# A hybrid decoder trunk on one core: the opening stage in strict order of its pieces, the squares of x behind it, and the statistics' product one chunk later

## The chip, the cores and the metric

The kernel runs on one core of a Trainium2 chip. The metric is the device time of one execution in microseconds (us). The engines are TensorE (PE in the profile, its weight loads PEld), VectorE (DVE), ScalarE (ACT), GpSimd (POOL) and SyncE (SP), which issues the DMAs here. Each engine works through its own queue in order.

## The reference

One layer, for a sequence of 256 positions and a width of 1024, all float32:

```
h    = rms_norm(x) * g_mix
proj = h @ w_in                      # columns: attention q,k,v; second attention q,k,v; rx, rgate; 3 gates
xr   = causal_dwconv(rx, width 4)    # the recurrent branch starts from the columns rx
...
x    = x + merged @ w_out
x    = x + (gelu(u_gate) * u_val) @ ffn_down     # u = conv3(rms_norm(x) @ ffn_up)
out  = rms_norm(x)
```

What matters here is the beginning: `rms_norm` divides every position by the root of the mean square over the 1024 channels, and the first columns of the product that the kernel takes are those of `rx`. The division by the root can be done after the product, since it is one factor for each position.

## The kernel before, in words

Everything is held transposed: 128 channels on the partitions, 256 positions along the free axis, so x is 8 tiles of 128 x 256, called k = 0 to 7. A float32 product is made of three matmuls on fp32r parts: each operand is split into a high part (a ScalarE copy that rounds) and a low part (a VectorE subtraction), and `mm3` (L109) adds high·high (L110), high·low (L111) and low·high (L112). So each tile of x needs a pair of instructions (`scaled_split`, L162: L164 on ScalarE, L165 on VectorE, called xgh and xgl), and each tile of weights needs one too (whi on ScalarE, wlo on VectorE).

The weights come in 77 chunks of 1 MB in the order ORDER. Chunks 0 and 1 are special: they hold the first half of the rx columns, cut by k, so that the work can begin when the first pieces of x and of the weights are there. SP issues those pieces alternately (L122 to L132): weights for k = 0, x for k = 0, and so on; from k = 2 on a DMA carries two k. Then come the parameters, chunk 2 (L86) and two small vectors. The raw chunks have three buffers; the split halves of chunks (1024 columns) have four.

The opening stage is the loop of L200: for every k, split x's tile k, split the 512 columns of weights of that k (L209, L210; in two parts for k = 0), and make 12 matmuls into two PSUM banks `rxb` (96 in all). Behind the loop stand, in program order: the split of chunk 2 (`split_to(6)`, L96 and L97, halves 4 and 5); the squares of x (`sumsq_bcast`, L186: four ScalarE instructions over two tiles each) and their sum (L188: two additions on GpSimd, then one on VectorE); the product of that sum with a matrix of ones (`sumsq_mm`, L194 and L195), which puts the sum over all channels on every partition; `rstd_of` (L169 to L173: one ScalarE and four VectorE instructions), which makes the factor `rstd1`; the evacuation of the two banks (`rx_evac`, L262), which multiplies by `rstd1`; and chunks 2 and 3 (`T_chunk`, 48 matmuls and one bank each), tied behind the statistics' product on TensorE. The pool of banks `psA` has four: rxb0, rxb1, then one for each chunk, so chunk 4 takes the bank of rxb0 again.

The order of the instructions on each engine is not that of the program. The framework schedules them: of what it thinks ready it takes what comes first in the program. The block `with tc.issue_after(i)` puts every instruction that it holds, and that runs on the engine of `i`, behind `i`. This sets an order on that engine and adds no wait on another one. In the kernel before, the opening loop has no such block, and the squares have none either. A chain of some 25 tiny GpSimd instructions over 8 columns (L290 to L304, tile `sm`) also runs in this stretch.

Of the kernel before, what the change touches and what calls it, by code (L numbers as in the profile page):

```python
# [8 lines left out]
F32 = mybir.dt.float32  # L9
F32R = mybir.dt.float32r  # L10
AF = mybir.ActivationFunctionType
ALU = mybir.AluOpType

P = 128
S = 256
D = 1024
KD = D // P
# [42 lines left out]
def hybrid_trunk(ctx: ExitStack, tc: tile.TileContext, x, wts, par, rgw, lqk, gf, out):  # L60
    nc = tc.nc
    V, A, G, T = nc.vector, nc.scalar, nc.gpsimd, nc.tensor
# [9 lines left out]
    def mm_bank(name):  # L72
        return psA.tile([P, 512], F32, name=name, tag="mm")

    def at_bank(name):
        return psB.tile([P, 512], F32, name=name, tag="at")


    raws, his, los = {}, {}, {}
    state = {"load": 0, "split": 0}  # L80

    def load_to(n):
        while state["load"] < min(n, NCHUNK):
            i = state["load"]
            raws[i] = rawp.tile([P, CH], F32, name=f"raw{i}", tag="raw")
            nc.sync.dma_start(raws[i], wts[i])  # L86
            state["load"] += 1

    def split_to(n):

        while state["split"] < min(n, 2 * NCHUNK):
            i = state["split"]
            raw = raws[i // 2][:, (i % 2) * HC:(i % 2 + 1) * HC]
            his[i] = wsp.tile([P, HC], F32R, name=f"whi{i}", tag="whi")
            los[i] = wsp.tile([P, HC], F32R, name=f"wlo{i}", tag="wlo")
            A.activation(his[i], raw, AF.Copy)  # L96
            V.tensor_tensor(los[i], raw, his[i].bitcast(F32), ALU.subtract)  # L97
            state["split"] += 1

    def half(i, e, name):  # L100
        assert ORDER[i][0] == name, (i, ORDER[i], name)
        load_to(i + RAW_BUFS)
        split_to(2 * i + e + W_BUFS)
        return his.pop(2 * i + e), los.pop(2 * i + e)
# [4 lines left out]
    def mm3(ps, wh, wl, ah, al, start, stop, **kw):  # L109
        T.matmul(ps, lhsT=wh, rhs=ah, start=start, stop=False, **kw)  # L110
        T.matmul(ps, lhsT=wh, rhs=al, start=False, stop=False, **kw)  # L111
        T.matmul(ps, lhsT=wl, rhs=ah, start=False, stop=stop, **kw)  # L112
# [4 lines left out]
    xt = xg_in[:, KD:].rearrange("p (k s) -> p k s", k=KD)  # L117
    gmix = xg_in[:, 0:KD]
# [20 lines left out]
    def pc(name, j, n=1):  # L139
        return par_s[:, PC[name] + j:PC[name] + j + n]  # L140
# [18 lines left out]
    xgh = big.tile([P, KD, S], F32R, name="xgh", tag="s1")  # L159
    xgl = big.tile([P, KD, S], F32R, name="xgl", tag="s2")  # L160

    def scaled_split(hi, lo, src, gain, ks):  # L162
        for k in ks:
            A.activation(hi[:, k, :], src[:, k, :], AF.Copy, scale=gain[:, k:k + 1])  # L164
            V.scalar_tensor_tensor(lo[:, k, :], src[:, k, :], gain[:, k:k + 1], hi[:, k, :].bitcast(F32),  # L165
                                   op0=ALU.mult, op1=ALU.subtract)

    def newton(y, m, t, r, ss_ap, scale):
        A.activation(y, ss_ap, AF.Abs_reciprocal_sqrt, bias=eps_s, scale=scale)  # L169
        V.tensor_scalar(m, ss_ap, -0.5 * scale, -0.5 * EPS, op0=ALU.mult, op1=ALU.add)  # L170
        V.tensor_tensor(t, y, y, ALU.mult)
        V.tensor_tensor(t, m, t, ALU.mult)
        V.scalar_tensor_tensor(r, t, 1.5, y, op0=ALU.add, op1=ALU.mult)  # L173

    def rstd_of(ss_ap, n, scale, name):

        m = work.tile([P, n], F32, name=name + "m", tag="nt_m", bufs=1)
        y = work.tile([P, n], F32, name=name + "y", tag="nt_y", bufs=1)
        t = work.tile([P, n], F32, name=name + "t", tag="nt_t", bufs=1)
        r = work.tile([P, n], F32, name=name + "r", tag="rstd", bufs=1)  # L180
        newton(y, m, t, r, ss_ap, scale)
        return r

    def sumsq_bcast(sq, k, src, name, later=False):

        A.activation(sq[:, k:k + 2, :], src[:, k:k + 2, :], AF.Square)  # L186
        if k:
            (G if k < 6 else V).tensor_tensor(sq[:, 0:2, :], sq[:, 0:2, :], sq[:, k:k + 2, :], ALU.add)  # L188
        if k == 6 and not later:
            return sumsq_mm(sq, name)  # L190

    def sumsq_mm(sq, name):
        ps = at_bank(name + "ss")
        T.matmul(ps[:, :S], lhsT=ones, rhs=sq[:, 0, :], start=True, stop=False)  # L194
        return ps[:, :S], T.matmul(ps[:, :S], lhsT=ones, rhs=sq[:, 1, :], start=False, stop=True)  # L195

    rx_banks = [mm_bank(f"rxb{b}") for b in range(2)]
    for k in range(KD):  # L200
        scaled_split(xgh, xgl, xt, gmix, [k])
        if k % 2 == 0:
            his[k // 2] = wsp.tile([P, HC], F32R, name=f"whi{k // 2}", tag="whi")
            los[k // 2] = wsp.tile([P, HC], F32R, name=f"wlo{k // 2}", tag="wlo")
        wh = his[k // 2][:, (k % 2) * 512:(k % 2 + 1) * 512]
        wl = los[k // 2][:, (k % 2) * 512:(k % 2 + 1) * 512]
        raw = raws[k // 4][:, (k % 4) * 512:(k % 4 + 1) * 512]
        for c in (slice(0, 256), slice(256, 512)) if k == 0 else (slice(0, 512),):
            A.activation(wh[:, c], raw[:, c], AF.Copy)  # L209
            V.tensor_tensor(wl[:, c], raw[:, c], wh[:, c].bitcast(F32), ALU.subtract)  # L210
        for t in range(4):
            mm3(rx_banks[t // 2][:, (t % 2) * S:(t % 2 + 1) * S], wh[:, t * P:(t + 1) * P], wl[:, t * P:(t + 1) * P],
                xgh[:, k, :], xgl[:, k, :], start=(k == 0 and t % 2 == 0), stop=(k == KD - 1 and t % 2 == 1),
                skip_group_check=True)
    state["split"] = 4
    load_to(4)
    split_to(6)
    sq1 = big.tile([P, KD, S], F32, name="sq1", tag="s7")
    for k in range(0, KD, 2):
        ss1 = sumsq_bcast(sq1, k, xt, "n1")  # L220
    ss1, ss1_mm = ss1
    rstd1 = rstd_of(ss1, S, 1.0 / D, "n1")
    gffn = pc("gffn", 0, 8)

    G.iota(dist, pattern=[[-1, S]], base=P, channel_multiplier=1, allow_small_or_imprecise_dtypes=True)
# [3 lines left out]
    def T_chunk(i, name, ah, al, evac, nk=KD, kouter=False):  # L229

        nt = HC // (nk * P)
        ps = None
        if kouter:
            hv = [half(i, e, name) for e in range(2)]
            ps = mm_bank(f"mm{i}")
            for k in range(KD):
                for t in range(2):
                    w = slice(k * P, (k + 1) * P)
                    mm3(ps[:, t * S:(t + 1) * S], hv[t][0][:, w], hv[t][1][:, w], ah[:, k, :], al[:, k, :],
                        start=(k == 0 and t == 0), stop=(k == KD - 1 and t == 1), skip_group_check=True)  # L240
            evac(ps, ORDER[i][1] * 2)
            return
        for e in range(2):
            wh, wl = half(i, e, name)
            wh4 = wh.rearrange("p (t k c) -> p t k c", k=nk, c=P)
            wl4 = wl.rearrange("p (t k c) -> p t k c", k=nk, c=P)
            for t in range(nt):
                o = (e * nt + t) % 2
                if o == 0:
                    ps = mm_bank(f"mm{i}_{e}{t}")  # L250
                for k in range(nk):
                    mm3(ps[:, o * S:(o + 1) * S], wh4[:, t, k, :], wl4[:, t, k, :],
                        ah[:, k, :], al[:, k, :], start=(k == 0), stop=(k == nk - 1))
                if o == 1:
                    evac(ps, ORDER[i][1] * 2 * nt + e * nt + t - 1)

    SP = S + 3
    rx = big.tile([P, KD, SP], F32, name="rx", tag="s5")
    G.memset(rx[:, :, 0:3], 0.0)

    def rx_evac(ps, t):
        V.tensor_tensor(rx[:, t:t + 2, 3:], ps.rearrange("p (t s) -> p t s", t=2),  # L262
                        rstd1[:, None, :].to_broadcast([P, 2, S]), ALU.mult)
# [10 lines left out]
        A.activation(hh[:, s, :], hf[:, s, :], AF.Copy)  # L274
        V.tensor_tensor(hl[:, s, :], hf[:, s, :], hh[:, s, :].bitcast(F32), ALU.subtract)

    rx_evac(rx_banks[0], 0)
    rx_evac(rx_banks[1], 2)
    pos = 2
    for c in range(2):  # L280
        with tc.issue_after(ss1_mm.ins):
            T_chunk(pos, "rx", xgh, xgl, rx_evac)
        pos += 1


    sm = const.tile([P, 12, 8], F32, name="sm")
# [398 lines left out]
    sq1 = big.tile([P, KD, S], F32, name="sq1b", tag="s1")  # L685
# [71 lines left out]
    for name, idx in FFN_ORDER:  # L757
        if name == "up":
            raw = idx < RAW_UP
# [11 lines left out]
        else:  # L771
# [3 lines left out]
            last = NFF // 2 - 1  # L775
# [7 lines left out]
            for h, c, i, e in ([(h, c, i, e) for h in range(2) for c in range(2) for i in (last - 1, last)  # L783
# [4 lines left out]
                ps = dn_banks[h][c]  # L788
# [81 lines left out]
```

## Time and profile before

| | |
|---|---|
| time, median of three runs | 483.67 us (483.54 to 484.66) |
| the profiled execution | 483.25 us, span 481.1 us |
| PE busy | 469.9 us (98%), 3580 matmuls |
| DVE busy | 382.6 us (80%) |
| ACT busy | 305.4 us (63%) |
| POOL busy | 19.7 us (4%) |
| mean granted TensorE clock | 0.997 of full speed |

The span begins and ends inside the execution, so its time is a little longer than the span. Busy time is that of instructions, so an engine that waits for a semaphore is idle. A matmul's end is modelled: matmuls overlap in the records (0.28 us each, starting 0.12 us apart), and the steady rate is read from their starts.

### The profile page before, as it was taken

The page shows a single profiled execution, that of the slowest core. Times are in us where ns is not written, and L with a number is a line of the kernel's source. Part 1 is how long each engine was busy: PE and PEld are TensorE (multiplying, and loading weights), DVE is VectorE, ACT ScalarE, POOL GpSimd, SP SyncE. Part 2 cuts the span into 40 slices and gives each one's busy share as a digit, 9 for nine tenths or more (in the row PEclk, how much of TensorE's full clock was granted, in tenths as well). Part 3 has the DMA queues.
Part 4 walks back from the last instruction along what each step waited for, and adds up shares of the span by engine and source line. Part 5 has one row for each costly group of instructions (what it writes and reads, how often), then busy time and mean ns, then how long its engine had stood idle before and what let it go on. Part 6 is the DMA issues. An engine that isn't in the chain of part 4 may idle for free.

```text
span 481.1 us, 8975 instructions
## 1 busy us (share of the span) xinstructions
PE 469.9 (98%) x3580; PEld 451.1 (94%) x3580; DVE 382.6 (80%) x686; ACT 305.4 (63%) x517; POOL 19.7 (4%) x46
## 2 busy tenths in 40 slices
PE   6999999999999999999999999999999999999994
PEld 5999999989999999999999999999999999999983
DVE  4899979657877599979567787999887788678575
ACT  6756739567778895576454556867565556555562
POOL 2640000000000000000000020000000000000000
PEclk9999999999999999999999999999999999999998
DMA  8954996998452525556654555455655445555302
GB/s 258 360 198 182 274 276 236 250 218 322 168 174 89 175 80 184 187 193 231 253 187 176 219 176 174 177 181 181 229 195 178 175 176 184 180 195 187 131 1 89
DMA packets 20395, 92.61 MB, mean 192 GB/s; under 512 B 1921, under 2 KB 8833, under 8 KB 10625
## 3 DMA queue, kind: packets, MB, share of 16 engines
q1 hardware_dynamic: 20352, 92.03, 56.2%
q8 instruction: 28, 0.46, 0.4%
q14 instruction: 15, 0.11, 0.1%
HBM read 84.69 MB, written 1.05 MB: 178 GB/s over the span
## 4 chain that ended last, share of the span: by engine, by line
PE 95%; ACT 1%; DMA 1%; DVE 1%; issue 0%; SPq 0%; DVEq 0%
PE mm L110 24%; PE mm L111 24%; PE mm L112 24%; PE dn L789 4%; PE dn L790 4%; PE dn L791 4%; DMA raw<-in_wts_dram 1%; PE va L450 1%; PE vc L448 1%; PE va L448 1%; PE va L449 1%; PE vc L450 1%; PE vc L449 1%; PE oa L498 0%; PE rxb L112 0%; PE rgg L110 0%
## 5 line engine op out<-in xcount | busy, mean ns | idle before, releaser
L96 ACT ACTIVATE whi<-raw 128x1024 fp32r<-128x1024 f32 x150 | 158.2, 1058 | 121.6 <-PE mm L111 87.1
L97 DVE TENSOR_TENSOR wlo<-raw,whi 128x1024 fp32r<-128x1024 f32 x150 | 182.6, 1220 | 50.6 <-ACT whi L96 49.1
L110 PE MATMUL mm<-x1h,whi 128*128 128x256 f32 x320 | 90.9, 284 | 0.0
L110 PE MATMUL mm<-hh,whi 128*128 128x256 f32 x320 | 90.9, 284 | 0.0
L112 PE MATMUL mm<-hh,wlo 128*128 128x256 f32 x320 | 90.5, 283 | 0.0
L111 PE MATMUL mm<-hl,whi 128*128 128x256 f32 x320 | 90.5, 283 | 0.0
L111 PE MATMUL mm<-x1l,whi 128*128 128x256 f32 x320 | 90.3, 282 | 0.0
L112 PE MATMUL mm<-x1h,wlo 128*128 128x256 f32 x320 | 89.7, 280 | 0.0
L110 PEld LDWEIGHTS mm<-hh,whi 128*128 128x128 f32 x320 | 61.3, 192 | 0.1
L111 PEld LDWEIGHTS mm<-hl,whi 128*128 128x128 f32 x320 | 61.3, 192 | 0.0
L112 PEld LDWEIGHTS mm<-hh,wlo 128*128 128x128 f32 x320 | 61.3, 192 | 0.0
L112 PEld LDWEIGHTS mm<-x1h,wlo 128*128 128x128 f32 x320 | 61.0, 191 | 0.0
L111 PEld LDWEIGHTS mm<-x1l,whi 128*128 128x128 f32 x320 | 60.7, 190 | 0.2
L110 PEld LDWEIGHTS mm<-x1h,whi 128*128 128x128 f32 x320 | 60.2, 188 | 0.2
L789 PE MATMUL dn<-whi,act 128*128 128x512 f32 x88 | 34.5, 392 | 0.0
L790 PE MATMUL dn<-wlo,act 128*128 128x512 f32 x88 | 34.4, 391 | 0.0
L791 PE MATMUL dn<-whi,act 128*128 128x512 f32 x88 | 34.3, 390 | 0.0
L110 PE MATMUL mm<-xgh,whi 128*128 128x256 f32 x96 | 27.0, 282 | 0.0
L111 PE MATMUL mm<-xgl,whi 128*128 128x256 f32 x96 | 26.9, 280 | 0.0
L112 PE MATMUL mm<-xgh,wlo 128*128 128x256 f32 x96 | 26.9, 280 | 0.0
L707 ACT ACTIVATE cv<-us,par_s 128x256 f32<-128x256 f32 x40 | 21.6, 588 | 0.0
L717 ACT ACTIVATE act<-cv 128x256 fp32r<-128x256 f32 x22 | 9.1, 412 | 17.4 <-DVE cv L713 17.4
(476 smaller groups left out, 1016.5 us busy)
## 6 DMA issues: line engine op xcount, KB each, us to landing
raw<-in_wts_dram SPq DMA_DIRECT2D x75, 1024.0 KB, 4.8
raw<-in_wts_dram SPq DMA_DIRECT2D x3, 512.0 KB, 6.6
KSa<-kha SPq DMA_DIRECT2D x4, 256.0 KB, 5.6
KLa<-qka SPq DMA_DIRECT2D x4, 256.0 KB, 6.3
KSc<-khc SPq DMA_DIRECT2D x4, 256.0 KB, 5.9
KLc<-klc SPq DMA_DIRECT2D x4, 256.0 KB, 8.7
rgw<-in_rgw_dram SPq DMA_DIRECT2D x2, 512.0 KB, 11.3
xt<-in_x_dram SPq DMA_DIRECT2D x1, 1024.0 KB, 7.1
```

The lines of the kernel that those rows point to most:

```text
L96: A.activation(his[i], raw, AF.Copy)
L97: V.tensor_tensor(los[i], raw, his[i].bitcast(F32), ALU.subtract)
L110: T.matmul(ps, lhsT=wh, rhs=ah, start=start, stop=False, **kw)
L111: T.matmul(ps, lhsT=wh, rhs=al, start=False, stop=False, **kw)
L112: T.matmul(ps, lhsT=wl, rhs=ah, start=False, stop=stop, **kw)
L448: T.matmul(banks[s], lhsT=hs, rhs=wh3[:, kk], start=(k == 0), stop=False)
L449: T.matmul(banks[s], lhsT=hs, rhs=wl3[:, kk], start=False, stop=False)
L450: T.matmul(banks[s], lhsT=ls, rhs=wh3[:, kk], start=False, stop=(k == 7))
L707: A.activation(cv[:, e, :], src[:, o:o + S], AF.Identity, bias=pc("fb", ch), scale=pc("fw", 88 + ch))
L789: T.matmul(ps, lhsT=hi, rhs=hv[i][e][0][:, o], start=(i == 0 and e == 0), stop=False)
L790: T.matmul(ps, lhsT=hi, rhs=hv[i][e][1][:, o], start=False, stop=False)
L791: T.matmul(ps, lhsT=lo, rhs=hv[i][e][0][:, o], start=False, stop=(i == last and e == 1))
```

## The change

Three things are altered. In the opening loop a list `last` holds the last ScalarE and the last VectorE instruction of the piece before, and the splits of piece k are issued behind them, so both engines take the pieces strictly in the order of k. The split of chunk 2 is put behind piece 7 and the squares behind the split of chunk 2 in the same way. And the statistics' product, with `rstd_of` and the evacuation of the two banks, moves behind the matmuls of chunk 2, whose own evacuation is kept in a list (`late`) and done after theirs; chunk 3 is tied behind the product.

```diff
@@ split_to @@
-            A.activation(his[i], raw, AF.Copy)
-            V.tensor_tensor(los[i], raw, his[i].bitcast(F32), ALU.subtract)
+            state["a"] = A.activation(his[i], raw, AF.Copy)
+            state["v"] = V.tensor_tensor(los[i], raw, his[i].bitcast(F32), ALU.subtract)
@@ opening stage @@
+    last = []
+
+    def behind():
+        es = ExitStack()
+        for i in last:
+            es.enter_context(tc.issue_after(i))
+        return es
+
     for k in range(KD):
-        scaled_split(xgh, xgl, xt, gmix, [k])
...
-        for c in (slice(0, 256), slice(256, 512)) if k == 0 else (slice(0, 512),):
-            A.activation(wh[:, c], raw[:, c], AF.Copy)
-            V.tensor_tensor(wl[:, c], raw[:, c], wh[:, c].bitcast(F32), ALU.subtract)
+        with behind():
+            scaled_split(xgh, xgl, xt, gmix, [k])
+            for c in (slice(0, 256), slice(256, 512)) if k == 0 else (slice(0, 512),):
+                a_ = A.activation(wh[:, c], raw[:, c], AF.Copy)
+                v_ = V.tensor_tensor(wl[:, c], raw[:, c], wh[:, c].bitcast(F32), ALU.subtract)
+        last[:] = [a_.ins, v_.ins]
...
     load_to(4)
-    split_to(6)
+    with behind():
+        split_to(6)
+    last[:] = [state["a"].ins, state["v"].ins]
     sq1 = big.tile([P, KD, S], F32, name="sq1", tag="s7")
-    for k in range(0, KD, 2):
-        ss1 = sumsq_bcast(sq1, k, xt, "n1")
-    ss1, ss1_mm = ss1
-    rstd1 = rstd_of(ss1, S, 1.0 / D, "n1")
+    with behind():
+        for k in range(0, KD, 2):
+            sumsq_bcast(sq1, k, xt, "n1", later=True)
...
-    rx_evac(rx_banks[0], 0)
-    rx_evac(rx_banks[1], 2)
     pos = 2
-    for c in range(2):
-        with tc.issue_after(ss1_mm.ins):
-            T_chunk(pos, "rx", xgh, xgl, rx_evac)
-        pos += 1
+    late = []
+    T_chunk(pos, "rx", xgh, xgl, lambda ps, t: late.append((ps, t)))
+    ss1, ss1_mm = sumsq_mm(sq1, "n1")
+    rstd1 = rstd_of(ss1, S, 1.0 / D, "n1")
+    for b, t in [(rx_banks[0], 0), (rx_banks[1], 2)] + late:
+        rx_evac(b, t)
+    pos = 3
+    with tc.issue_after(ss1_mm.ins):
+        T_chunk(pos, "rx", xgh, xgl, rx_evac)
+    pos = 4
```

## Rows read from the trace of the kernel before

**Rows 1.** Window 21 to 60: length, busy us (instructions) of each engine, PE clock, DMA share, GB/s.

```profile
21.00:60.00 39.00, 39.00 (x312) 38.09 (x311) 36.68 (x62) 25.78 (x34) 7.75 (x18) 1.00 0.68 233
```

**Rows 2.** All waits of PE in the span: us in total, times, longest.

```profile
PE rxb L110 <- ACT whi L209: 2.1, 3, 1.0
PE warm L147 <- DVE eps_s L149: 1.0, 1, 1.0
PE rxb L112 <- DVE wlo L210: 0.8, 2, 0.7
```

**Rows 3.** Timeline of PE: start, us, engine, line, operation, tiles, [idle before <- releaser].

```profile
11.76 0.39 PE L112 MATMUL rxb<-xgh,wlo 128*128 128x256 f32 x1 [0.67 <-DVE wlo L210]
...
14.36 0.28 PE L111 MATMUL rxb<-xgl,whi 128*128 128x256 f32 x1
14.80 0.39 PE L112 MATMUL rxb<-xgh,wlo 128*128 128x256 f32 x1 [0.16 <-DVE wlo L210]
...
20.36 0.60 PE L194 MATMUL n1ss<-sq,ones 128*128 128x256 f32 x2
...
21.35 0.28 PE L111 MATMUL mm<-xgl,whi 128*128 128x256 f32 x1
...
32.50 0.28 PE L110 MATMUL mm<-xgh,whi 128*128 128x256 f32 x1
```

**Rows 4.** Timeline of ACT in the opening.

```profile
8.66 1.14 ACT L186 ACTIVATE sq<-xg_in 128x512 f32<-128x512 f32 x2
9.70 1.14 ACT L209 ACTIVATE whi<-raw 128x512 fp32r<-128x512 f32 x2
10.74 0.89 ACT L164 ACTIVATE xgh<-xg_in 128x256 fp32r<-128x256 f32 x2
...
12.06 1.14 ACT L209 ACTIVATE whi<-raw 128x512 fp32r<-128x512 f32 x2
...
14.42 1.13 ACT L209 ACTIVATE whi<-raw 128x512 fp32r<-128x512 f32 x2
...
16.71 2.01 ACT L96 ACTIVATE whi<-raw 128x1024 fp32r<-128x1024 f32 x2 [0.82 <-DMA raw<-in_wts_dram]
18.74 1.28 ACT L169 ACT_TABLE_LOAD   x1
21.43 0.47 ACT L169 ACTIVATE n1y<-n1ss,eps_s 128x256 f32<-128x256 f32 x1 [1.40 <-PE n1ss L195]
```

**Rows 5.** Timeline of DVE in the opening, single instructions and pairs.

```profile
10.35 1.36 DVE L210 TENSOR_TENSOR wlo<-raw,whi 128x512 fp32r<-128x512 f32 x1 [1.01 <-ACT whi L209]
...
12.63 1.52 DVE L165 SCALAR_TENSOR_TENSOR xgl<-xg_in,xgh 128x256 fp32r<-128x256 f32 x1
14.07 1.28 DVE L210 TENSOR_TENSOR wlo<-raw,whi 128x512 fp32r<-128x512 f32 x2
15.28 0.87 DVE L165 SCALAR_TENSOR_TENSOR xgl<-xg_in,xgh 128x256 fp32r<-128x256 f32 x2
...
18.01 1.21 DVE L97 TENSOR_TENSOR wlo<-raw,whi 128x1024 fp32r<-128x1024 f32 x1
...
25.70 1.28 DVE L262 TENSOR_TENSOR rx<-rxb,n1r 128x512 f32<-128x512 f32 x2
```

**Rows 6.** Timeline of POOL.

```profile
9.88 1.28 POOL L188 TENSOR_TENSOR sq<-sq 128x512 f32<-128x512 f32 x1 [6.97 <-ACT sq L186]
...
12.30 1.57 POOL L188 TENSOR_TENSOR sq<-sq 128x512 f32<-128x512 f32 x1 [1.08 <-ACT sq L186]
...
18.15 1.13 POOL L292 TENSOR_TENSOR sm<-sm 128x8 f32<-128x8 f32 x1 [1.90 <-DVE lam_s L314]
...
30.05 0.23 POOL L304 TENSOR_SCALAR sm<-sm 128x8 f32<-128x8 f32 x1
```

**Rows 7.** SP's issue of the weights for k = 2 and 3.

```profile
3.53 0.43 SPq L132 DMA_DIRECT2D raw<-in_wts_dram  x1
```

**Rows 8.** DMA issues at 3.5 to 3.9: size, us from issue to landing.

```profile
raw<-in_wts_dram SPq DMA_DIRECT2D x1, 512.0 KB, 5.6
```

## The prediction

> **What bounds the kernel now.** I read the stretches first, then what PE waits for, then the timelines of the opening. From 21 us on PE is busy without a gap at full granted clock, 39.00 of 39 us in the first such stretch [rows 1], and the list of PE's waits over the whole span names nothing but the opening: 2.1 us for high parts of weights, 0.8 us for low parts, 1.0 us before the warm-up [rows 2]. So PE sets the end, and after the opening every later matmul follows the one before. A microsecond that the opening gives PE comes out at the end, as long as no new wait takes it; work taken from ACT, DVE or POOL elsewhere is worth nothing.
>
> In the opening, the reader should look at the two matmuls that begin after a wait for a low part, at 11.76 and 14.80 us [rows 3]. From 14.80 to the statistics' product at 20.36 there are the last 46 of the 96 matmuls: 5.56 us, that is 46 at 0.1185 and 0.11 for the restart. From 11.76 to 14.36 the same rate gives 22 more starts and the next one would have come at 14.48. So 68 matmuls follow 11.76, and 28 (k = 0, 1 and four of k = 2) came before.
>
> Why is the low part of k = 2 late? Two reasons. ACT makes two squares, 8.66 to 9.80, while the weights for k = 2 and 3 (issued at 3.53, landed 5.6 later, at 9.13) lie ready; their high part begins at 9.70 instead [rows 4, 7, 8]. And DVE needs 1.36 us for the low part, 10.35 to 11.71, where a free one takes 0.68 (a pair 1.28, so 0.60 apart) [rows 5]: GpSimd's addition of those squares runs from 9.88 to 11.16 [rows 6]. The second addition, 12.30 to 13.87, does the same to the x part of k = 5 (1.52 us; a free pair takes 0.87) and makes the low weights of k = 4 late, the wait at 14.80.
>
> **The change: the opening.** Four squares (0.52 apart) leave ACT's opening and three additions leave POOL's and DVE's; nothing is added there, and no DMA is moved. ACT begins the high part of k = 2 at 9.15 and ends it at 9.77; DVE makes the low part at 9.79 to 10.47, and PE goes on at 10.52 (it started 0.05 after the low part's end before) instead of 11.76: 1.24 us. For k = 3, ACT needs 0.52 and 0.40 more, so its high part ends at 10.69 and the low one at 11.47; PE wants that at 10.52 + 0.11 + 8 x 0.1185 + 0.24 = 11.82. The pieces k = 4 and 5 follow at 1.00 us each on DVE (0.60 + 0.40) against PE's 1.42, so the margin grows, as long as the weights have landed. They had by 12.06 for k = 4 and by 14.42 for k = 6, where ACT took them straight after other work [rows 4]; from there the low parts would be ready at 13.35 and 15.71, and PE wants them at 13.24 and 16.08. For k = 4 that latest case costs 0.2; I take none, since 12.06 stood behind a square. So the wait at 14.80 goes too: 14.80 - 14.48 + 0.11 = 0.43. PE ends the opening at 10.52 + 0.11 + 68 x 0.1185 = 18.69 instead of 20.36: **1.67 us**. Bounds: nothing, if PE meets another late piece; and 2.1 us, if it had all four late matmul groups of k = 2 in hand and lost neither the wait nor the restart.
>
> **The change: chunk 2 comes too early.** Its weights do not come earlier: ACT stood idle 0.82 us for their landing and began at 16.71 [rows 4]. One high half takes 1.06, its low part on a free DVE 1.21 [rows 5]: 17.79 to 19.00, at PE 19.05. PE, now without the statistics in between, wants the first low part with the third matmul of chunk 2, at 18.69 + 2 x 0.1185 = 18.93. So it stands 0.12 and restarts for 0.11: **0.23 us given back**. That landing is a ceiling: however soon the opening ends, chunk 2 can't pass 19.05 with its third matmul. Only another order of chunk 2's matmuls, high parts first, would lift it; then up to the whole 1.67 stays. The chunk's rate is (32.50 - 21.35)/95 = 0.1174 [rows 3], so its 48 matmuls are through at 19.05 + 0.23 + 45 x 0.1174 = 24.56.
>
> **The change: the statistics.** The product costs the same at its new place: from 20.36 to the second matmul of the next chunk at 21.35 are 0.99 us where 0.12 are due, so 0.87 before and after. What must hold is that the sum of squares is there by 24.56. ACT ends half 5 at 18.72 and then squares: the second ends near 19.8, the fourth near 20.8. GpSimd's first addition finds DVE on the low part of half 5 (18.95 to 20.16); the two additions then take 20.2 to 22.7 at 1.28 each, and DVE's addition ends at 23.4. If DVE puts one split of chunk 3 (1.21) ahead of it, 24.5. Either is just in time: **0**, with bounds of 0 and about 1.1 us (two splits ahead, 25.7).
>
> The Trainium skill, "SBUF — State Buffer", section "Who interferes with whom", says that a VectorE instruction with two SBUF inputs and a GpSimd instruction that reads SBUF exclude each other wholly, whoever comes first. The trace agrees: the low part of k = 2 ends 0.55 us after GpSimd's addition, and the second addition took 1.57 behind a VectorE instruction instead of 1.28 [rows 5, 6]. By that rule GpSimd waits for half 5 as I have it; were they to share, half 5 would be some 0.4 us later, before PE needs it near 22, so the sum stays at 0 either way.
>
> Then the factor: from the product's end, ACT's root began at 21.43, which is 1.07 after 20.36, and the first bank was free at 25.70 + 0.68 = 26.38 [rows 4, 5], 4.95 us later. Now: 24.56 + 1.07 = 25.63 and 30.58. Chunk 4 takes that bank at 24.56 + 0.87 + 48 x 0.1174 = 31.07. It holds by 0.5 us: **0**; bounds 0 and 0.7 (one more split of 1.21 in between). The third evacuation and the later weight splits are covered by PE's chunks of 5.6 us. The table load in front of the root (1.28 us [rows 4]) lies in ACT's time before 25.63.
>
> **Sum.** 1.67 - 0.23 - 0 - 0 = 1.44 us off the profiled execution's 483.25, so 481.81. The median of the runs is 0.42 above it, so 483.67 - 1.44 = 482.23. That is 0.30% under the time before, and 0.3% (1.45 us) is about what a measurement of this kernel can tell from no change. The likeliest case lies on that line.
>
> **Rivals.**
>
> 1. *The statistics' product waits.* GpSimd or DVE take other work ahead of the additions, as the tiny chain that has one of 1.13 us at 18.15 [rows 6]. PE then stands before chunk 3. One or two such pieces: 0.3 to 1.4 us lost, 482.5 to 483.6. For it: the margin is 0.1 to 1.2 us. Against it: the additions come first in the program.
> 2. *Chunk 2 is ordered with its high parts first*, or its landing is a little earlier: 1.67 to 2.0 us gained, 481.7 to 482.0. For it: four matmuls of k = 2 stood ahead of its first low one. Against it: at k = 4, where 46 of 48 follow the wait at 14.80, the low one stands third again.
> 3. *The bank is late.* The root is held up and chunk 4 waits for bank 0. A delay of 1.2 us on ACT or DVE costs 0.7: 482.9. The Trainium skill, "ScalarE: Activation LUTs", section "What ACT_TABLE_LOAD costs", counts about 2.66 us with the drain for a switch of tables; the row shows 1.28 with 0.02 before it, and if the load cost as the page has it, 1.38 more would leave this rival's loss at up to 0.9.
> 4. *Slower: GpSimd runs the whole tiny chain first.* It lasted from 18.15 to 30.28 [rows 6]. With two additions and DVE's behind it, the sum would come near 33.5, the product 9 us late, and the time be 7.5 us above the one before, 491. It decides from a sum later than 24.56 + 1.44 = 26.0. Against it: two squares are ready near 19.8, 1.7 us after that row, and of what is ready the earlier in the program is taken; it comes true only if the scheduler's idea of that moment is far off.
> 5. *No change:* a piece other than the squares holds PE, and the opening ends near 20.3: 483.7.
>
> **How the numbers follow.** The forecast (481.8 to 482.7 alone) 0.50; rival 1, 0.20; rival 2, 0.11; rival 3, 0.06; rival 4 and other losses beyond 0.3%, 0.09; rival 5, 0.04. Faster by over 0.3%: rival 2 and a little over half of the forecast, 0.39. Slower 0.09. Within 0.3%: the rest, 0.52. The range 481.3 to 484.0 holds all but rival 4 and takes in the spread of the runs.
>
> **What the profile would show.** ACT takes xgh, whi of each k in turn with no square before 18.7; whi of k = 2 begins near 9.15; no low split in the opening is over 0.7 us; PE's wait at 14.80 is gone and its last rxb matmul starts near 18.6; a short wait for L97 stands at 19; the product starts near 24.6 without a wait and chunk 4 near 31.1. A wait of the product for DVE's addition speaks for rival 1 or 4, one of chunk 4 for L262 for rival 3, none at 19 for rival 2. The prediction is wrong if GpSimd's additions don't stand right behind the squares, or if a raw landing has moved.

## The result and the profile after

The changed kernel is slower: 487.23 us in the median of 22 runs (484.92 to 488.75), beside 484.39 for the kernel before on the same chips; the ratio is 1.0054, with an interval of 1.004 to 1.0068. The ratios here and below are taken over the fast runs of both kernels, so they differ a little from the quotients of the medians. The prediction was 482.2, with a range of 481.3 to 484.0. Rival 4, which had a chance of 0.09 with its like, is what happened, at a lower price than its 491. The profiled execution took 487.29 us with a span of 485.2 and a mean granted clock of 0.994, against 483.25, 481.1 and 0.997 before.

All waits of PE in the kernel after, as [rows 2] (us in total, times, longest):

```profile
PE n1ss L194 <- DVE sq L188: 3.5, 1, 3.5
PE rxb L110 <- ACT whi L219: 1.2, 2, 0.9
PE warm L147 <- DVE eps_s L149: 1.0, 1, 1.0
```

The opening's own waits have shrunk: the low parts (0.8 us before) are gone from the list and the high parts fell from 2.1 to 1.2. But a new wait of 3.5 us stands at the head, and it is the statistics' product that waits for VectorE's addition. The lines of the split are now L219 and L220 (L209 and L210 before), the tiny chain is L307 to L321 (L290 to L304 before). The timeline of PE, as [rows 3]:

```profile
10.60 0.38 PE L112 MATMUL rxb<-xgh,wlo 128*128 128x256 f32 x1
...
18.86 0.28 PE L112 MATMUL rxb<-xgh,wlo 128*128 128x256 f32 x1
18.98 0.28 PE L110 MATMUL mm<-xgh,whi 128*128 128x256 f32 x1
...
19.25 0.38 PE L112 MATMUL mm<-xgh,wlo 128*128 128x256 f32 x1
...
24.63 0.28 PE L112 MATMUL mm<-xgh,wlo 128*128 128x256 f32 x1
28.43 0.70 PE L194 MATMUL n1ss<-sq,ones 128*128 128x256 f32 x2 [3.52 <-DVE sq L188]
```

Up to 24.63, the last matmul of chunk 2, things go nearly as the prediction had them: PE goes on at 10.60 (10.52 forecast), chunk 2's first low part is in use at 19.25 (19.05), and chunk 2 is through at 24.63 + 0.12 = 24.75 (24.56). Then PE stands still. Who is late is seen on three engines. ACT, as [rows 4], makes the high part of k = 2 at 9.19 with no square in front, and its squares right behind chunk 2's high parts:

```profile
9.19 0.63 ACT L219 ACTIVATE whi<-raw 128x512 fp32r<-128x512 f32 x1 [0.94 <-DMA raw<-in_wts_dram]
...
16.87 2.01 ACT L96 ACTIVATE whi<-raw 128x1024 fp32r<-128x1024 f32 x2 [1.08 <-DMA raw<-in_wts_dram]
18.79 2.18 ACT L186 ACTIVATE sq<-xg_in 128x512 f32<-128x512 f32 x4
...
29.93 0.47 ACT L169 ACTIVATE n1y<-n1ss,eps_s 128x256 f32<-128x256 f32 x1 [2.75 <-PE n1ss L195]
```

The four squares are done at 20.97. POOL, as [rows 6], doesn't take them up:

```profile
16.78 0.20 POOL L309 TENSOR_TENSOR sm<-sm 128x8 f32<-128x8 f32 x1 [0.32 <-DVE sm L308]
...
18.23 1.02 POOL L313 TENSOR_TENSOR sm<-sm 128x8 f32<-128x8 f32 x1
19.34 1.08 POOL L314 TENSOR_SCALAR sm<-sm 128x8 f32<-128x8 f32 x1
20.51 0.20 POOL L313 TENSOR_TENSOR sm<-sm 128x8 f32<-128x8 f32 x1
...
24.73 0.23 POOL L321 TENSOR_SCALAR sm<-sm 128x8 f32<-128x8 f32 x1
25.04 2.61 POOL L188 TENSOR_TENSOR sq<-sq 128x512 f32<-128x512 f32 x2
```

It runs the tiny chain to its end at 24.96 and only then the two additions, though the last of all squares was there 4 us earlier. DVE, as [rows 5], shows the end of the delay:

```profile
9.86 0.69 DVE L220 TENSOR_TENSOR wlo<-raw,whi 128x512 fp32r<-128x512 f32 x1 [1.09 <-ACT whi L219]
...
16.49 0.20 DVE L308 RECIPROCAL sm<-sm 128x8 f32<-128x8 f32 x1
17.96 2.37 DVE L97 TENSOR_TENSOR wlo<-raw,whi 128x1024 fp32r<-128x1024 f32 x2 [1.27 <-ACT whi L96]
27.68 0.69 DVE L188 TENSOR_TENSOR sq<-sq 128x512 f32<-128x512 f32 x1 [7.35 <-POOL sq L188]
```

VectorE's own addition stands in its queue ahead of the splits of chunk 3, so the engine waits 7.35 us for POOL and the whole queue stands with it. And there is a second loss behind the first. Stretches of the span (length, busy time and count of PE, PEld, DVE, ACT and POOL, granted clock, DMA share, GB/s):

```profile
26.00:28.00 2.00, 0.00 (x0) 0.00 (x0) 0.32 (x1) 1.19 (x1) 1.57 (x2) 1.00 0.03 12
28.00:29.00 1.00, 0.57 (x3) 0.52 (x4) 1.00 (x2) 0.00 (x0) 0.00 (x0) 1.00 0.00 0
29.00:32.00 3.00, 3.00 (x14) 2.82 (x13) 3.00 (x4) 0.47 (x1) 0.00 (x0) 0.51 0.09 11
32.00:33.00 1.00, 1.00 (x9) 1.00 (x8) 1.00 (x2) 0.00 (x0) 0.00 (x0) 0.75 0.80 270
33.00:60.00 27.00, 27.00 (x228) 26.91 (x227) 26.36 (x47) 18.05 (x25) 0.00 (x0) 1.00 0.65 213
```

From 29 to 32 us PE is busy all the time, but the granted clock is 0.51, the lower of its two levels (1.2 GHz), and 14 matmuls start where a full clock has room for 26. Before the fall the engine had stood still for 3.52 us. From 33 on the clock is full and PE busy without a gap, as in [rows 1].

**Where the time went.** By the starts of PE's last matmul (473.59 before, 478.04 after) the loss is 4.45 us. Chunk 2 is through at 24.75 instead of 26.87 - 0.87 = 26.00, if the product that lay before it is taken out: 1.25 gained. The product starts at 28.43 instead of 24.75: 3.68 lost. From the product to the last matmul are 449.61 us, where the first experiment below, at full clock, has 447.95: 1.66 lost. Nearly all of it lies in the first chunk: from the product's start to that of the 48th matmul behind it are 8.10 us here and 6.45 there. The remaining 0.36 lies in the later chunks (before has 453.23 - 48 x 0.1174 = 447.59), and the tail behind the last matmul is 0.35 shorter, so the two nearly cancel in the span.

### The profile page after: what moved, and what is told of

It reads as the page before. It is cut to its first block, busy times and chain, and to the rows that moved or that the text cites. A ratio compares the mean times of both kernels' runs of the same rounds, so it can differ in the third digit from the quotient of the medians.

```text
span 485.2 us, 8979 instructions
## 1 busy us (share of the span) xinstructions
PE 472.6 (97%) x3580; PEld 453.5 (93%) x3580; DVE 381.0 (79%) x686; ACT 305.5 (63%) x517; POOL 15.6 (3%) x46
## 4 chain that ended last, share of the span: by engine, by line
PE 93%; POOL 2%; DMA 2%; ACT 1%; SPq 1%; DVE 1%; issue 1%; DVEq 0%; POOLq 0%
PE mm L110 23%; PE mm L111 23%; PE mm L112 23%; PE dn L806 4%; PE dn L807 4%; PE dn L808 4%; DMA raw<-in_wts_dram 2%; PE va L465 1%; PE vc L466 1%; PE vc L467 1%; PE va L466 1%; PE vc L465 1%; PE va L467 1%; POOL sq L188 1%; POOL sm L314 1%
## 5 line engine op out<-in xcount | busy, mean ns | idle before, releaser
L110 PE MATMUL mm<-xgh,whi 128*128 128x256 f32 x96 | 28.0, 291 | 0.0
```

## The experiments

Each ran beside runs of the kernel before on the same chip. Two reasons for the loss were to be told apart: POOL's order, with the chain in front of the additions (theory A), and something in the new place of the product or the strict order itself (rival). The first two experiments keep the strict order and the later product as they are and alter only the order of POOL's work or the engine of the additions.

**The chain behind the additions.** The changed kernel, with the whole block of the tiny chain tied behind GpSimd's last addition.

```diff
+            state["g" if k < 6 else "s"] = (G if k < 6 else V).tensor_tensor(
+                sq[:, 0:2, :], sq[:, 0:2, :], sq[:, k:k + 2, :], ALU.add)
...
+    with tc.issue_after(state["g"].ins):
+        A.activation(sm[:, 0], lam_c, AF.Abs)
...
```

> The changed kernel, with the chain of small GpSimd instructions (tile sm) put behind GpSimd's second addition of squares; nothing else moves. Theory A (the loss is GpSimd's queue: the additions stood behind the whole chain, PE waited 3.52 us for the sum, and the clock then fell): the additions run at about 20 to 22.7 us, the sum is there by 24.5, PE's product starts near 24.75 without a wait, the clock stays full, and the time is 1.0 to 1.4 us under the kernel before (ratio 0.997 to 0.998), some 4 us under the changed kernel. Rival B (the later product itself costs, by the factor and the banks coming late, whoever makes the sum): PE's wait moves to chunk 4 and the kernel stays 1 us or more slower than before.

Measured: 482.03 us (481.03 to 482.80, 12 runs) beside 484.79 (482.96 to 489.87, 33 runs); ratio 0.9925, interval 0.9896 to 0.9953. POOL's timeline of this run, and below it PE's:

```profile
20.25 2.85 POOL L188 TENSOR_TENSOR sq<-sq 128x512 f32<-128x512 f32 x2 [17.29 <-ACT sq L186]
```

```profile
25.00 0.59 PE L195 MATMUL n1ss<-sq,ones 128*128 128x256 f32 x2
```

The additions come 4.8 us earlier, the product runs without a wait, and the granted clock is 1.00 from 24 to 60 us. The loss is gone, and the gain of the opening is seen. The ratio is lower than the 0.997 to 0.998 that was expected, since the runs of before spread far upwards; the two profiled executions, 482.19 and 483.25, lie 1.06 us apart, as expected. Against the changed kernel the gain is plain: the slowest run here, 482.80, is below its fastest, 484.92.

**All additions on VectorE.** The changed kernel again; now the chain keeps its place at the head of POOL, and the additions leave POOL.

```diff
-            (G if k < 6 else V).tensor_tensor(sq[:, 0:2, :], sq[:, 0:2, :], sq[:, k:k + 2, :], ALU.add)
+            (V if name == "n1" else G if k < 6 else V).tensor_tensor(
+                sq[:, 0:2, :], sq[:, 0:2, :], sq[:, k:k + 2, :], ALU.add)
```

> The changed kernel, with all three additions of the first statistics on VectorE; the chain stays where it is on GpSimd. Theory A: VectorE, which stood idle from 20.3 to 27.7 us, adds at 0.68 us each behind the squares, the sum is there near 21.6, no wait at the product, full clock, ratio 0.997 to 0.998 as with the chain moved. If the port between GpSimd and VectorE were the cause and not the order of GpSimd's queue, the chain beside it would still make the additions late, and a wait of 1 us or more stays.

Measured: 481.73 (480.71 to 481.86, 10 runs), ratio 0.9912, interval 0.9878 to 0.9946. This is the fastest version of the study, and its slowest run lies below the fastest of the 33 of before. DVE and PE in this run:

```profile
20.14 2.27 DVE L188 TENSOR_TENSOR sq<-sq 128x512 f32<-128x512 f32 x3
22.38 3.73 DVE L97 TENSOR_TENSOR wlo<-raw,whi 128x1024 fp32r<-128x1024 f32 x3
```

```profile
24.71 0.59 PE L195 MATMUL n1ss<-sq,ones 128*128 128x256 f32 x2
```

The chain was as early as in the changed kernel and did no harm, so it is its place in front of the additions, not the chain, that cost the time. Two edits that have only this in common both win back more than the loss, with the strict order and the later product in place and no wait of chunk 4 in either run: theory A stands, and the rival falls.

**The wait filled with matmuls.** To price the clock by itself: the changed kernel with 14 matmuls of `ones` by `ones` between chunk 2 and the product. They are work added, and their result isn't used.

```diff
...
-    ss1, ss1_mm = sumsq_mm(sq1, "n1")
+    fill = at_bank("fill")
+    with tc.issue_after(state["mm"].ins):
+        for _ in range(14):
+            fl = T.matmul(fill[:, 0:P], lhsT=ones, rhs=ones, start=True, stop=True)
+    with tc.issue_after(fl.ins):
+        ss1, ss1_mm = sumsq_mm(sq1, "n1")
...
```

> The changed kernel, with 14 matmuls of ones by ones (128 columns, result unused) between chunk 2 and the statistics' product, so that PE works through most of its wait of 3.5 us. The sum comes as late as before. Theory A1 (the 3.4 us at half clock after the wait are a price of PE's idleness): the clock stays full and the time falls by about 1.7 us against the changed kernel (half of 3.4). Rival (the slow matmuls behind the wait come from something else, such as the float32 product itself or VectorE's four splits at that time): they stay slow, and the time stays that of the changed kernel.

Measured: 486.58 (485.71 to 490.42, 12 runs), ratio 1.0036, interval 1.0004 to 1.0067. Its stretch from 29 to 32 us, and its waits of PE:

```profile
29.00:32.00 3.00, 3.00 (x27) 3.00 (x26) 3.00 (x4) 0.57 (x2) 0.00 (x0) 1.00 0.17 44
```

```profile
PE a0s L484 <- issue: 1.2, 1, 1.2
...
PE n1ss L194 <- DVE sq L188: 0.4, 1, 0.4
```

The clock stays full and 27 matmuls start instead of 14. But much less than 1.66 us is seen in the time, since PE now meets the attention scores (L484) 1.2 us too early. The profile names no releaser for this wait; the copies of `KSa`, which the scores read, took 8.2 us from issue to landing, against 5.5 in the changed kernel (medians of four), and are the likeliest one. So the same kernel ran once more, on another chip, beside the changed one:

> The changed kernel with 14 matmuls of ones in the wait, unchanged from the first such run, on the same chip. There the clock stayed full, but the gain of 1.7 us was all but eaten by a wait of 1.23 us before the first attention scores at 70 us, behind a copy of k on the DMA queues that took 8.2 us. Theory A1 with that second wait being a consequence (the factor comes late, so q and k, their copies and the scores do): the wait at the scores is there again, 0.5 to 1.5 us, and the time 0.3 to 0.9 us under the changed kernel. Rival: that copy was slow by chance; the wait is absent and the time is about 1.7 us under the changed kernel, 485 to 485.6.

> The changed kernel, unchanged, on the same chip as the kernel before and the filled wait. Theory A: GpSimd's additions again start behind the chain, near 25 us, PE waits 3.4 to 3.6 us at the product, half clock follows for about 3.4 us: 486.5 to 487.5. If the half clock is chance, it may lack here, and the time is then 1.5 to 2 us lower or the wait moves elsewhere.

Measured: filled 486.23 (485.34 to 490.16, 10 runs), changed 487.31 (486.21 to 488.11, 10 runs), before 485.04; ratios to before 1.0023 (0.9991 to 1.0054) and 1.0046 (1.0018 to 1.0075). The changed kernel again shows the 3.5 us wait, the half clock behind it and 449.62 us from product to last matmul. In the filled one this is 448.18, with a short wait for a bank in it and without that for the scores, which theory A1 had expected again; this execution took 485.34, 1.74 under the changed kernel's 487.08, and is the fastest of its ten. From the product's start to that of the 48th matmul behind it, both profiles of the changed kernel take 8.10 us and both of the filled one, which still wait 0.4 us at the product, 6.58. So the fall of the clock costs about 1.5 us of PE's time; 1.1 is what the medians show.

**The squares ahead of chunk 2's split.** Why did the chain come first at all? In the program the additions stand ahead of it. Theory: the scheduler counts on the squares late, since they are tied behind the split of chunk 2, which waits for a landing. The changed kernel with the squares moved ahead of that split (and the factor tied behind it):

```diff
-    with behind():
-        split_to(6)
-    last[:] = [state["a"].ins, state["v"].ins]
     sq1 = big.tile([P, KD, S], F32, name="sq1", tag="s7")
     with behind():
         for k in range(0, KD, 2):
             sumsq_bcast(sq1, k, xt, "n1", later=True)
+    split_to(6)
...
```

> The changed kernel with the squares ahead of the split of chunk 2 on ACT instead of behind it, and the factor's instructions put behind the splits of chunk 3's halves on ACT and VectorE. Theory A2 (the chain came first on GpSimd because the squares stood behind chunk 2's landing, which the scheduler expects later than it comes): the two additions come before the chain without any order given to GpSimd, at about 16 to 19 us, the product waits for nothing, full clock. The squares now delay chunk 2's first high part from 16.9 to about 17.4, so PE waits about 0.7 us at chunk 2: 482.3 to 483.2, faster than before by 0.1 to 0.3%. Rival: the additions stand early and the time is still above before, so the loss was not GpSimd's queue.

Measured: 483.25 (482.25 to 483.80, 10 runs), ratio 0.9951, interval 0.9922 to 0.9981. POOL, then PE:

```profile
16.73 2.65 POOL L188 TENSOR_TENSOR sq<-sq 128x512 f32<-128x512 f32 x2 [1.73 <-ACT sq L186]
19.88 0.34 POOL L307 TENSOR_SCALAR sm<-sm 128x8 f32<-128x8 f32 x1 [0.48 <-ACT sm L306]
```

```profile
20.17 0.70 PE L194 MATMUL n1ss<-sq,ones 128*128 128x256 f32 x2 [1.27 <-DVE sq L188]
```

The additions are now in front of the chain, without any order given to POOL. But the edit moved the chain too: the second of the two ScalarE instructions that feed it came at 19.60, behind the split of chunk 2, where the changed kernel has it at 15.58, ahead of it. So the run shows that the places of squares and feeders around that split decide POOL's order. It doesn't part the two, and that the scheduler counts with an expected landing is the likeliest reading, and argued. The edit had a side effect that nobody had asked for: the product went back to its old place behind the opening's 96 matmuls, where PE waited 1.27 us for the sum; a product without a wait had been expected.

**The parts alone.** From the kernel before: only the strict order of the loop's pieces (first diff below); the same with all additions on VectorE; and only the later product.

```diff
...
     for k in range(KD):
-        scaled_split(xgh, xgl, xt, gmix, [k])
...
+        with behind():
+            scaled_split(xgh, xgl, xt, gmix, [k])
...
+        last[:] = [a_.ins, v_.ins]
```

> The kernel before, with the strict order of the pieces in the opening loop alone: squares, additions and product where the scheduler puts them, the product right behind the opening. Theory A: the order gains in the opening and nothing is lost behind it. Two squares fall into ACT's wait for the weights of k = 2 and their addition on GpSimd still holds up the low part of k = 2, so the opening ends near 19.3 (before 20.36, the changed kernel 18.7), and chunk 2 is late enough for its weights: 0.8 to 1.2 us under the kernel before (ratio 0.9975 to 0.9985), a product without a wait. Rival C (the order itself costs, since it forbids ACT and VectorE to take what is ready): no gain or a loss.

Measured: 483.36 (482.55 to 485.23, 12 runs), ratio 0.9951, interval 0.9921 to 0.9981. The squares stay in the opening here, and DVE's timeline shows what that costs:

```profile
9.54 1.36 DVE L219 TENSOR_TENSOR wlo<-raw,whi 128x512 fp32r<-128x512 f32 x1 [1.08 <-ACT whi L218]
...
11.36 0.68 DVE L219 TENSOR_TENSOR wlo<-raw,whi 128x512 fp32r<-128x512 f32 x1
11.96 1.52 DVE L165 SCALAR_TENSOR_TENSOR xgl<-xg_in,xgh 128x256 fp32r<-128x256 f32 x1
```

Two splits still take 1.36 and 1.52 us, as in [rows 5]. The opening's 96th matmul starts at 19.58, against 20.25 before and 18.86 in the changed kernel: the strict order has about half of the gain, the squares' removal the other half. This is one profile of each, and the landings move the end of the opening too (20.80 in a second profile of the kernel before), so the halves are rough. The two long splits agree with what the Trainium skill says ("SBUF — State Buffer", "Who interferes with whom"): VectorE with two inputs in SBUF and GpSimd reading there shut each other out.

```diff
-            (G if k < 6 else V).tensor_tensor(sq[:, 0:2, :], sq[:, 0:2, :], sq[:, k:k + 2, :], ALU.add)
+            (V if name == "n1" else G if k < 6 else V).tensor_tensor(
+                sq[:, 0:2, :], sq[:, 0:2, :], sq[:, k:k + 2, :], ALU.add)
```

> The strict order alone (product at its old place, squares free), with the three additions on VectorE. In the run with the strict order alone, GpSimd's two additions still held up two instructions of VectorE (1.36 and 1.52 us) and PE waited 0.9 us for low parts. Theory A (that hold-up was the rest of the opening's loss): VectorE's additions cost it 0.6 us each but hold up nothing, the opening ends 0.3 to 0.8 us earlier than there, and the product behind it covers chunk 2's landing: 481.8 to 482.6. Rival: three more instructions on VectorE in the opening make the low parts as late as GpSimd did, and the time stays at that of the strict order alone (483.4).

Measured: 482.80 (481.27 to 485.62, 12 runs), ratio 0.9951, interval 0.9921 to 0.9981; the 96th matmul at 19.45, only 0.13 earlier than with the strict order alone. Without POOL's addition the low part of k = 2 takes 0.68, but VectorE's own addition of 0.69 now stands in front of it. Yet in this profile a tile of x landed late: ScalarE waited 1.20 us for it, to 8.46, and made the high part of k = 2 at 9.92, 1.03 us later than in the run before. So what the change of engine by itself is worth in the opening isn't shown.

```diff
-        ss1 = sumsq_bcast(sq1, k, xt, "n1")
-    ss1, ss1_mm = ss1
+        sumsq_bcast(sq1, k, xt, "n1", later=True)
...
+    T_chunk(pos, "rx", xgh, xgl, lambda ps, t: late.append((ps, t)))
+    ss1, ss1_mm = sumsq_mm(sq1, "n1")
...
```

> The kernel before with only the third part of the change: the statistics' product, the factor and the evacuations one chunk later; no strict order, squares and additions where they were. The additions then end by 16.8 us, long before the product. Theory A (the chain on GpSimd is the whole loss) in its simplest form says no wait at the product and a time within 0.3% of before. But the queues of this kernel have ACT's root and VectorE's first three factor instructions ahead of the splits of chunk 3, and those now wait for the later product (near 26 us): worked out from the rows, the first low part of chunk 3 comes near 30.1 where PE wants it at 27.2, a new wait of about 3 us for L97, perhaps with half clock behind it (1 to 1.7 us): 487 to 488. Rival B (a later product is harmless by itself): 483.5 to 484.5.

Measured: 484.12 (483.27 to 489.09, 10 runs), ratio 0.9980, interval 0.9945 to 1.0016: no change that can be told. The run did not test what it was made for. PE's timeline:

```profile
21.65 0.28 PE L111 MATMUL mm<-xgl,whi 128*128 128x256 f32 x1
21.77 0.59 PE L194 MATMUL n1ss<-sq,ones 128*128 128x256 f32 x2
```

The product stands behind two matmuls of chunk 2, not behind 48: here, where the sum is early, the scheduler took the product early, whatever its place in the program. What the later product does by itself stays open.

**The floor at 19 us.** The prediction held that chunk 2 can't pass 19.05 with its third matmul, whatever the opening does, because a half's two splits lie behind the landing. The version with all additions on VectorE, with the first half of chunk 2 split in two pieces of 512:

```diff
-            state["a"] = A.activation(his[i], raw, AF.Copy)
-            state["v"] = V.tensor_tensor(los[i], raw, his[i].bitcast(F32), ALU.subtract)
+            for c in (slice(0, 512), slice(512, HC)) if i == 4 else (slice(0, HC),):
+                state["a"] = A.activation(his[i][:, c], raw[:, c], AF.Copy)
+                state["v"] = V.tensor_tensor(los[i][:, c], raw[:, c], his[i][:, c].bitcast(F32), ALU.subtract)
```

> The changed kernel with the additions on VectorE, and the first half of chunk 2 split in two pieces of 512 columns on ACT and VectorE, so that its first low part is ready 0.5 to 0.6 us after the high one begins to be read instead of 1.2. The prediction had chunk 2's landing as a ceiling that gives 0.23 us back. Theory: the wait at 19 us goes, and the time falls by 0.2 to 0.4 us against the kernel with the additions on VectorE (481.7). Rival: the wait had been hidden in PE's queue and nothing changes (within 0.1 us).

Measured: 482.44 (481.97 to 484.02, 12 runs), ratio 0.9943, interval 0.9915 to 0.9970. The product starts at 24.29, 0.42 us earlier than with the additions on VectorE. Of this, 0.17 is an opening that ended earlier in this profile; the other 0.25 is the wait at 19, which is gone (0.23 forecast). The timelines of DVE and PE show who takes it back:

```profile
29.15 1.23 DVE L98 TENSOR_TENSOR wlo<-raw,whi 128x1024 fp32r<-128x1024 f32 x1 [0.65 <-ACT whi L97]
30.29 0.42 DVE L174 SCALAR_TENSOR_TENSOR n1r<-n1t,n1y 128x256 f32<-128x256 f32 x1
30.75 1.29 DVE L276 TENSOR_TENSOR rx<-rxb,n1r 128x512 f32<-128x512 f32 x2
```

```profile
31.58 0.35 PE L111 MATMUL mm<-xgh,whi 128*128 128x256 f32 x1 [0.63 <-DVE rx L276]
```

Chunk 4 waits 0.63 us for its bank. That isn't for the earlier chunk alone. The root came at 26.74, 1.38 later behind the product than forecast, for the table load ran from 25.45 to 26.73, behind the last split; and VectorE takes a split of weights (L98) ahead of the factor's last instruction (L174). So the first evacuation (L276) begins at 30.75; the version with all additions on VectorE, whose root was as late but had no split there, has it at 29.38. The floor was there, and right behind it stands rival 3: the root held up. The fall of 0.2 to 0.4 us that was expected isn't seen in the times.

**The kernel before again**, for the spread of its runs:

> The kernel before, unchanged, profiled once more and timed against itself. In the profile of the kernel with the later product alone, whose opening has the same instructions in the same order as the kernel before, the granted clock was half for 3.4 us from about 12.8 us, in the middle of the opening, behind PE's waits for weights. Theory D: the kernel before has the same hazard, and its runs above 485 us are of that kind. A profiled execution is then either like the first (full clock to the end, last matmul near 473.6 us in the span) or has 3.4 us at half clock in the opening and ends 1.5 to 2 us later. Rival: the half clock there was a matter of the moved product; then the opening stays at full clock in any profile of this kernel. Against itself the ratio is 1 within 0.5%.

Measured: 484.55 (483.32 to 485.22, 10 runs), ratio 0.9968, interval 0.9936 to 0.9999, for a kernel against itself. So a ratio of 0.997 is no result here, and the ratios of 0.994 and 0.995 above, of four versions whose medians are only 0.2 to 0.4% under those of the kernel before, are hardly more; what is read from these runs is read from their timelines. No half clock stood in its opening; why runs of before reach 493.72 where those of the two best versions stay within 1.8 us stays open.

## Why the prediction was wrong

**The opening held.** The high part of k = 2 at 9.19 (9.15 forecast), its low part in 0.69 us, PE on at 10.60, the wait at 14.80 gone, the end at 18.98 instead of 18.69. The 0.29 is 0.08 at the start and about 0.2 at the low part of k = 4, the latest case that was named and taken as none. One count was loose without effect: 67 matmuls follow the one at 11.76, and the 68th start is that of the product.

**Chunk 2 held.** The floor was real, as the run with the pieces of 512 shows. Its landing was 0.16 later than before (16.87 for 16.71), so the third matmul came at 19.25 and the chunk's end at 24.75. As the opening ended later too, only about 0.13 of the 0.23 was given back. Opening and chunk 2 together gained 1.25 us where 1.44 were forecast.

**The step that failed is "The change: the statistics".** It let the two additions run from 20.2 to 22.7, right behind the squares, and so took the delay of the sum as 0 with a bound of 1.1 us. They ran from 25.04 to 27.65, the sum came at 28.37, and PE lost 3.68 us. The prediction had named this as the sign of being wrong: additions that don't stand right behind the squares. The reason given against rival 4, that "of what is ready the earlier in the program is taken", asks what is ready on the chip. But POOL began pieces of the chain from 20.51 to 24.73, when the first two squares were there since about 19.9 and all four since 20.97: it follows an order fixed beforehand. That the chain was ready first in the scheduler's reckoning, so that the exception ("only if the scheduler's idea of that moment is far off") held, fits this and is argued. The step in the change that likely brings it about is the squares tied behind a split that waits for a landing; the run with the squares ahead of that split, which also put the chain's feeder behind it, undid the order.

**Rival 4's price was off in both directions.** Its sum near 33.5 came at 28.37. The reciprocal in front of the chain ran at 16.49, so POOL's first product began at 16.78, and not at 18.15; and from there to its end the chain took 8.2 us, not 12.1. The rows show why: the two instructions of over 1 us stand beside VectorE's splits (17.96 to 20.33), and the others, beside an idle VectorE, took 0.20 to 0.24. The very wait that the chain caused made it faster. Against this, the fall of the clock, about 1.5 us, was in no case of the prediction.

**What else was forecast.** Rival 3 did not come, neither after nor in the two mended versions, but its term of 0 was right by luck. With all additions on VectorE the table load ran from 25.86 to 27.14, between the last split and the root, and not before it, so the root came at 27.16, 1.38 later behind the product than forecast. In return VectorE had no split between the root and the first evacuation: the bank was free 2.9 us behind the root, and not 4.95. With a split there, in the run with the pieces of 512, the bank came 4.7 us behind a root as late, and chunk 4 waited 0.63, where the bound was 0.7. Rival 2 did not come: chunk 2's low part stood third. The sum itself was near: the profiled execution took 482.19 us in the version that has the additions where the step had them (the chain behind them) and 481.82 with all of them on VectorE, for 481.81. That the second agrees to 0.01 is luck: by the start of PE's last matmul the two gain only 0.64 and 0.90 us of the 1.44, and the tail behind it, which is in no term of the sum, is 0.4 us shorter in both.

## What to carry to other kernels

When a producer is moved behind something that waits for a landing, read for each engine that its consumers use which other work could be put ahead of them, and tie that work behind them or give the consumers another engine; the place in the program alone didn't decide the order here. A gap on the engine that sets the end may cost more than its own length, as the one of 3.52 us did here by about 1.5: look at the granted clock in the stretch that follows it. And a mended experiment that gains says more than a filled wait, whose gain the next wait can take.

## What the runs showed of the hardware

After the product's wait of 3.52 us (3.46 in the second profile) the granted clock was 0.51 (0.50) from 29 to 32 us with PE busy throughout, in both profiled executions of the changed kernel; with the wait filled, in two more, it was 1.00. The same level was seen once more while PE was at work: in the run with the later product alone, in an opening whose order of instructions is that of before. PE had waited 0.93 us there, to 10.51, and 0.66 us, to 11.90. Its stretches:

```profile
12.00:14.00 2.00, 2.00 (x13) 2.00 (x14) 2.00 (x3) 2.00 (x5) 1.55 (x1) 0.70 1.07 432
14.00:16.00 2.00, 2.00 (x11) 2.00 (x11) 2.00 (x5) 1.97 (x6) 1.36 (x2) 0.50 1.03 422
```

Neither profile of the kernel before shows it, though the second has waits of 1.16 and 0.66 us in its opening, so what brought it on is open. A GpSimd instruction on 8 columns took 0.20 us beside an idle VectorE and 1.01 to 1.13 beside one that was splitting weights (kernels before and after), five times as much for work of the same size.
